# Undivided softmax weights, a four-block first modulation and a 12-tile ring in a two-block, four-layer network on one Trainium2 core

## The chip, the core and the metric

One core of one Trainium2 (trn2) chip runs the whole program. The core has a matmul engine (PE, with its weight loads PEld), three engines for everything elementwise (DVE, ACT, POOL), a queue engine (SP) from which every transfer of this kernel is issued, in order, and 16 DMA engines that serve it. The metric is the device time of one execution in microseconds (us), lower is better. Times below are medians of several runs or come from one profiled execution, and the text says which.

## What is computed

Two blocks, each of two layers, over a sequence of 1024 tokens of width 1024; in the first block also 256 context tokens. The change touches the first block: its modulations and its attention. Cut to those:

```
def hybrid_layer(xl, xc, c, c_ctx, w_mod, b_mod, ...):          # twice; the second without the context's update
    shift, scale, gate = split(silu(c) @ w_mod + b_mod, 3)       # 1024 -> 3072
    mod_c = silu(c_ctx) @ w_mod[:, :n] + b_mod[:n]
    hl = rms_norm(xl) * (1 + scale) + shift;   hc = the same of xc with mod_c
    pl = hl @ w_in;   pc = hc @ w_in
    a = conv_branch(...)                        # gated convolution of 31 taps
    b = windowed_attention(q, k, v, kc, vc, sink) * silu(b_gate)
    c = gated linear attention in chunks of 64
    xl = xl + gate * (concat(a, b, c) @ w_out)  # the context likewise in the first layer

def one_block(qn, kn, vn, mn):                  # 128 queries; 8 heads on 2 key heads
    s_loc = where(mn, qn . kn, -1e30);   s_ctx = qn . kc;   s_sink = sink
    p = softmax(concat([s_sink, s_ctx, s_loc]))
    return p_ctx . vc + p_loc . vn
```

The second block (gated spatial unit, pooling, retention, a feed-forward net with a short convolution) is untouched.

## The kernel before

Activations lie feature-major, [128 features, tokens], in three groups ("keys"): tokens 0 to 511, tokens 512 to 1023, and the 256 of the context. Projections are exact to float32 by splitting: each operand is a rounded part (`hi`) and a rest (`lo`), and each product is three matmuls of 512 columns (`mm3`, lines 226 to 228) over eight slices k of the inner dimension. A weight tile arrives as `wraw` (line 213, a ring of 3), ACT rounds it to `whi` (line 214), DVE makes `wlo` (line 201).

The program is written in stages, and a scheduler interleaves them: it fixes the order of the instructions of each engine and of SP's transfers when the program is built. On the chip every engine and every queue then works its list in that order, and waits where something isn't ready. Matmuls inside `in_order()` stay together.

**Start (`run`, lines 1653 to 1666).** SP loads the first key's eight `x` tiles. `mods` (lines 362 to 389) makes the modulation of layer 0: `w_mod` comes in tiles `wm` of 256 KB (line 374), and the matmul of line 375 adds each to the strip of 32 output rows of its block, so that the blocks of a group lie in different strips of one PSUM bank. Then the bank is copied to `mrow` (line 378), transposed (line 381), and biases are added (lines 385, 389) into `mc`. The blocks of layer 0 are taken in the order `MO` = 2, 0, 3, 1 in groups of `MG` = 2, with `WM` = 8 tiles in the ring. Blocks 2 and 0 hold scale and shift of the slices 0 to 3, so that after the first group `operands` (lines 1640 to 1650) can begin with four of the eight slices: `hi` on ACT (line 1647), the modulated `x` on POOL (line 1648), `lo` on DVE (line 1649). Then the first projections start.

**Attention (`attention`, `attend`, lines 866 to 958).** For each block of 128 queries and each of 2 key heads (20 iterations in layer 0, of which the first 4 are the context's; 16 in layer 1): the scores of 4 heads go to PSUM (matmuls of lines 897 and 908), DVE adds the mask, moves them to `P` and takes the maximum (lines 901, 911), ACT takes the exponential with its sum (line 918), DVE inverts the sums (`rsm`, line 920), and the weights are divided by them (line 926) on the engines that `NV` names: heads 0 and 2 on DVE, 1 and 3 on POOL. One iteration later (`LA` = 1) `attend` transposes `P` (line 940, four to a bank; copies to `pt` by lines 943 and 945 on DVE and ACT), multiplies by the values (line 954) into `po`, copies `po` to `ot` (line 957) and stores it (line 958). Transposes and `po` share the three banks of `psA`.

**Around it.** After `layer1(0, ...)` the text has the second call of `mods` (line 1669): eight blocks in two groups of four, with 4 tiles in the ring, and after that `out_proj`, which multiplies the stored branches `yl`, times the gates `gl`, by `w_out` (lines 974 to 993: two tiles each of `yl` and `gl` in the ring, the product on line 987, `yhi` on line 990). The scheduler had drawn the second modulation, and the first loads of `out_proj`, into the attention of layer 0. The pools of `mods` and of `out_proj` open in the same stretch of memory, one after the other.

Of the kernel before, what the change touches and what calls it, by code (L numbers as in the profile page):

```python
# [9 lines left out]
F32 = mybir.dt.float32  # L10
# [3 lines left out]
ALU = mybir.AluOpType  # L14
# [4 lines left out]
D = 1024  # L19
# [8 lines left out]
MO = (2, 0, 3, 1)  # L28
WM = 8
MG = 2  # L30
# [23 lines left out]
NV = "DPDP"  # L54
# [35 lines left out]
class Net:  # L90
# [270 lines left out]

    def mods(self, blocks, bufs=4, MG=4):

        nc = self.nc
        pool, tag = (self.psC, "sc") if blocks[0] == (0, 2) else (self.psB, "ax")
        with self.right(f"wm{blocks[0][0]}{blocks[0][1]}", bufs) as wm:
            for o in range(0, len(blocks), MG):
                grp = blocks[o:o + MG]

# [6 lines left out]
                n = 32 * len(grp)  # L376
# [489 lines left out]
    def attention(self, l, maskr, kh, vst):  # L866
        nc, tc, I = self.nc, self.tc, self.I
        with tc.tile_pool(name=f"at{l}", bufs=2, reuse_waits="tile") as ap:
            blocks = [("c", 0), ("c", 1)] if l == 0 else []
            blocks += [("l", i) for i in range(8)]  # L870
            late = []
            for kind, i in blocks:
# [8 lines left out]
                for v in range(2):  # L881
# [34 lines left out]
                    rs = self.sm.tile([128, 4], F32, name="rsm")  # L916
# [4 lines left out]
                    for h in range(4):  # L921
                        if NV[h] == "A":
                            nc.scalar.mul(P[:, h, :n], P[:, h, :n], rs[:, h:h + 1])
                            continue
                        eng = nc.vector if NV[h] == "D" else nc.gpsimd
                        eng.tensor_scalar(P[:, h, :n], P[:, h, :n], rs[:, h:h + 1], 1.0, op0=ALU.mult, op1=ALU.mult)
                    late.append(lambda v=v, i=i, P=P, nkt=nkt, lo_t=lo_t, yd=yd: self.attend(ap, vst, v, i, P, nkt, lo_t, yd))
# [5 lines left out]
    def attend(self, ap, vst, v, i, P, nkt, lo_t, yd):  # L933
# [15 lines left out]
        po = self.psA.tile([128, 512], F32, name="mm", tag="mm")  # L949
        with self.in_order():  # L950
            for kt in range(nkt):
                vt = kt if kt < 2 else 2 + lo_t + kt - 2
                for u in range(2):
                    nc.tensor.matmul(po[half[u], :256], vst[:, vt, 64 * v:64 * v + 64], PT[kt][:, u * 256:u * 256 + 256],  # L954
                                     start=kt == 0, stop=kt == nkt - 1)
        ot = ap.tile([128, 2, 128], F32, name="ot", bufs=2)
        nc.scalar.copy(ot, po[:, :256].rearrange("p (m t) -> p m t", m=2))
        nc.sync.dma_start(out=yd[2 + 2 * v:4 + 2 * v, :, i * 128:i * 128 + 128].rearrange("m p t -> p m t"), in_=ot)
# [647 lines left out]
    def run(self):  # L1606
# [7 lines left out]
        with self.norm_scratch("x0"), self.right("x0") as xp:  # L1614
# [40 lines left out]
            self.mods([(0, j) for j in MO], WM, MG)  # L1655
# [13 lines left out]
        self.mods([(0, 4), (0, 5), (1, 4), (1, 5)] + [(1, j) for j in range(4)])  # L1669
# [172 lines left out]
```

## Time and profile before

| | us |
|---|---|
| median of 3 runs (3587.53 to 3593.46) | 3589.61 |
| the profiled execution | 3592.81 |
| its span, first to last instruction | 3590.8 |
| PE busy in it | 3424.5 (95%) |
| DVE busy | 2487.3 (69%) |
| ACT busy | 1209.4 (34%) |
| POOL busy | 632.3 (18%) |

All times in rows are counted from the start of the span. "L375" is line 375 of the kernel; `out<-in` are the tiles; an arrow in brackets gives what ended the wait before an instruction. A float32 matmul of lines 375 and 954 shows as two records. Matmuls overlap, so their durations add up to more than the time they take: what one costs is read from the distance between starts. The granted clock of PE stands as a share of 2.4 GHz.

### The profile page before, as it was taken

What the parts mean: (1) busy time and instruction counts of PE and PEld (TensorE: products, weight loads), DVE (VectorE), ACT (ScalarE), POOL (GpSimd) and SP (SyncE); (2) the same over time, 40 slices, a digit from 0 to 9 for tenths busy, and PEclk for the clock granted to TensorE, in tenths of its full rate; (3) what the DMA queues carried; (4) which work ended last, traced back from release to release, by engine and by line L of the source; (5) the groups of instructions that cost most, each with busy time, mean ns of one, the idle gap of its engine ahead of it and who ended that gap; (6) DMA issues with size and microseconds to landing.
All of it is one profiled execution on the core that took longest, in us unless ns stands there. A gap on an engine that the chain in (4) does not pass through costs nothing.

```text
span 3590.8 us, 46973 instructions
## 1 busy us (share of the span) xinstructions
PE 3424.5 (95%) x17414; PEld 2727.1 (76%) x17414; DVE 2487.3 (69%) x3933; ACT 1209.4 (34%) x2189; POOL 632.3 (18%) x548
## 2 busy tenths in 40 slices
PE   7979999998989999999999998999999999999998
PEld 4868766787876677887788877887887878777786
DVE  5866568567665856455699999447354599999545
ACT  4114246341242642223343343214113343333322
POOL 4011332000214220130123231000030032322000
PEclk9989999999998999999999999999999999999999
DMA  6232355533124244315222223425323522221532
GB/s 204 71 82 67 112 165 168 169 123 95 58 78 119 71 124 138 97 42 184 80 97 77 82 77 110 140 82 160 91 61 114 159 74 77 77 82 63 179 100 91
DMA packets 245972, 380.70 MB, mean 106 GB/s; under 512 B 29104, under 2 KB 103792, under 8 KB 245232
## 3 DMA queue, kind: packets, MB, share of 16 engines
q1 hardware_dynamic: 245744, 377.71, 33.8%
q8 instruction: 137, 2.24, 0.3%
q14 instruction: 91, 0.75, 0.1%
HBM read 280.35 MB, written 97.26 MB: 105 GB/s over the span
## 4 chain that ended last, share of the span: by engine, by line
PE 68%; DVE 16%; issue 6%; DMA 4%; ACT 3%; POOL 2%; SPq 1%; DVEq 0%; POOLq 0%; ACTq 0%
PE mm L226 13%; PE mm L228 13%; PE mm L227 13%; PE ax L226 3%; PE ax L228 3%; PE ax L227 3%; PE sc L226 3%; PE sc L227 3%; PE sc L228 3%; DVE wlo L201 2%; DVE cv L1463 2%; PE mm L954 2%; PE mm L940 2%; DVE fth L347 1%; PE ax L715 1%
## 5 line engine op out<-in xcount | busy, mean ns | idle before, releaser
L226 PE MATMUL mm<-hi,whi 128*128 128x512 f32 (+1 forms) x1780 | 689.9, 388 | 28.3 <-ACT whi L214 13.1
L228 PE MATMUL mm<-hi,wlo 128*128 128x512 f32 (+1 forms) x1780 | 686.2, 386 | 9.0 <-DVE wlo L201 9.0
L227 PE MATMUL mm<-lo,whi 128*128 128x512 f32 (+1 forms) x1780 | 685.6, 385 | 1.4 <-DVE lo L1649 1.1
L214 ACT CAST whi<-wraw 128x512 fp32r<-128x512 f32 (+3 forms) x412 | 232.4, 583 | 598.7 <-PE mm L227 261.5
L226 PEld LDWEIGHTS mm<-hi,whi 128*128 128x128 f32 x1780 | 337.4, 190 | 100.3 <-ACT whi L214 14.4
L228 PEld LDWEIGHTS mm<-hi,wlo 128*128 128x128 f32 x1780 | 336.5, 189 | 83.7 <-DVE wlo L201 14.5
L227 PEld LDWEIGHTS mm<-lo,whi 128*128 128x128 f32 x1780 | 337.3, 189 | 72.8 <-DVE lo L1649 3.1
L201 DVE TENSOR_TENSOR wlo<-wraw,whi 128x512 fp32r<-128x512 f32 (+3 forms) x412 | 269.4, 670 | 176.3 <-ACT whi L214 174.9
L226 PE MATMUL sc<-hi,whi 128*128 128x512 f32 x732 | 287.9, 393 | 12.5 <-ACT whi L214 10.6
L228 PE MATMUL sc<-hi,wlo 128*128 128x512 f32 x732 | 287.7, 393 | 2.1 <-DVE wlo L201 1.9
L227 PE MATMUL sc<-lo,whi 128*128 128x512 f32 x732 | 287.2, 392 | 2.6 <-DVE lo L1649 2.5
L226 PE MATMUL mm<-whi,hi 128*128 128x512 f32 (+2 forms) x704 | 262.2, 372 | 28.2 <-ACT whi L214 28.2
L227 PE MATMUL mm<-wlo,hi 128*128 128x512 f32 (+2 forms) x704 | 257.6, 366 | 0.3
L228 PE MATMUL mm<-whi,lo 128*128 128x512 f32 (+2 forms) x704 | 257.1, 365 | 0.0
L188 POOL TENSOR_TENSOR rs<-rs,mhalf 128x4 f32<-128x4 f32 (+1 forms) x19 | 19.5, 1028 | 1073.7 <-DVE rs L183 1073.7
L498 DVE SCALAR_TENSOR_TENSOR ca<-u,wh,ca 128x1024 f32<-128x1024 f32 (+1 forms) x180 | 187.8, 1044 | 2.9
L226 PE MATMUL ax<-hi,whi 128*128 128x512 f32 x456 | 180.0, 395 | 4.7 <-DVE xn L1378 4.7
L228 PE MATMUL ax<-hi,wlo 128*128 128x512 f32 x456 | 179.7, 394 | 2.9 <-DVE wlo L201 2.9
L227 PE MATMUL ax<-lo,whi 128*128 128x512 f32 x456 | 179.1, 393 | 0.0
L201 DVE TENSOR_TENSOR wlo<-wr,whi 128x512 fp32r<-128x512 f32 x200 | 174.0, 881 | 0.0
L226 PEld LDWEIGHTS sc<-hi,whi 128*128 128x128 f32 x732 | 138.2, 189 | 44.0 <-ACT whi L214 11.3
L226 PEld LDWEIGHTS mm<-whi,hi 128*128 128x128 f32 x704 | 134.3, 191 | 47.4 <-ACT whi L214 29.0
(367 smaller groups left out, 6588.3 us busy)
## 6 DMA issues: line engine op xcount, KB each, us to landing
wr<-in_w_up SPq DMA_DIRECT2D x80, 512.0 KB, 3.6
wraw<-in_w_fm SPq DMA_DIRECT2D x108, 256.0 KB, 3.0
wm<-in_w_mod SPq DMA_DIRECT2D x96, 256.0 KB, 3.7
wraw<-in_w_down SPq DMA_DIRECT2D x96, 256.0 KB, 2.8
hid_d<-fth SPq DMA_DIRECT2D x44, 512.0 KB, 2.6
wraw<-hid_d SPq DMA_DIRECT2D x88, 256.0 KB, 2.9
wraw<-in_w_out SPq DMA_DIRECT2D x80, 256.0 KB, 3.4
yl<-y_d SPq DMA_DIRECT2D x64, 256.0 KB, 3.2
```

The source lines that it names most:

```text
L188: nc.gpsimd.tensor_tensor(out, out, e, op=ALU.pow)
L201: nc.vector.tensor_sub(out, x, f(hi))
L214: nc.scalar.copy(hi[:, c], r)
L226: nc.tensor.matmul(ps, sh, mh, start=start, stop=False)
L227: nc.tensor.matmul(ps, sh, ml, start=False, stop=False)
L228: self.mark = nc.tensor.matmul(ps, sl, mh, start=False, stop=stop)
L347: nc.vector.scalar_tensor_tensor(out, tanh_tmp, 1.0, x, op0=ALU.add, op1=ALU.mult)
L498: self.not_before(nc.vector.scalar_tensor_tensor(a, u[:, j:j + n], wh[:, c, j:j + 1], a, op0=ALU.mult, op1=ALU.add))
L715: nc.tensor.matmul(o_, a_, b_, start=first_, stop=last_)
L940: nc.tensor.transpose(pt[:, j * 128:j * 128 + 128], P[:, h, kt * 128:kt * 128 + 128], self.ident)
L954: nc.tensor.matmul(po[half[u], :256], vst[:, vt, 64 * v:64 * v + 64], PT[kt][:, u * 256:u * 256 + 256], start=kt == 0, stop=kt == nkt - 1)
L1463: nc.vector.scalar_tensor_tensor(t[:, o:], x[:, 0:S - o], wc(2 - o), t[:, o:], op0=ALU.mult, op1=ALU.add)
```

## The change

Three edits. (1) `attend` gets `rs`, the inverted sums. The division of line 926 is gone; instead POOL spreads `rs` to 64 columns for each head (`rw`), PE transposes that in two pieces into the free half of the bank of `po`, and DVE multiplies `ot` by it after ACT's copy. (2) `MG` is gone: the first modulation takes its four blocks as one group. (3) Both calls of `mods` get a ring of `WM` = 12 tiles (before: 8 and 4).

```diff
@@ -26,8 +26,7 @@
 W2 = (3, 1)
 W3 = ()
 MO = (2, 0, 3, 1)
-WM = 8
-MG = 2
+WM = 12
 LP_FFN = 1
 LAG_C = 3
 LAG_P = 4
@@ -51,7 +50,6 @@
 Y1B = 1
 QB = 3
 PB = 5
-NV = "DPDP"
 PBF = 4
 PD = (1, 3)
 RT = 2
@@ -359,13 +357,13 @@
         nc.vector.tensor_scalar_mul(self.cs[:, :, 0:2], th, 0.5)
         self.mc = [self.const.tile([128, 2, 24], F32, name=f"mc{l}") for l in range(2)]
 
-    def mods(self, blocks, bufs=4, MG=4):
+    def mods(self, blocks, bufs=4):
 
         nc = self.nc
         pool, tag = (self.psC, "sc") if blocks[0] == (0, 2) else (self.psB, "ax")
         with self.right(f"wm{blocks[0][0]}{blocks[0][1]}", bufs) as wm:
-            for o in range(0, len(blocks), MG):
-                grp = blocks[o:o + MG]
+            for o in range(0, len(blocks), 4):
+                grp = blocks[o:o + 4]
 
                 ps = pool.tile([128, 512], F32, name=tag, tag=tag)
                 for k in range(8):
@@ -913,24 +911,19 @@
                                     scalar=mx[:, 0, h:h + 1], op0=ALU.add, op1=ALU.max, accum_out=mx[:, 1, h:h + 1])
                     nm = self.sm.tile([128, 4], F32, name="nm")
                     nc.vector.tensor_scalar_mul(nm, mx[:, 1 if nl else 0, :], -0.125)
-                    rs = self.sm.tile([128, 4], F32, name="rsm")
+                    rs = self.sm.tile([128, 4], F32, name="rsm", bufs=6)
                     for h in range(4):
                         nc.scalar.activation(P[:, h, :n + 1], P[:, h, :n + 1], AF.Exp, scale=0.125, bias=nm[:, h:h + 1],
                                              accum_out=sums[:, h:h + 1])
                     nc.vector.reciprocal(rs, sums)
-                    for h in range(4):
-                        if NV[h] == "A":
-                            nc.scalar.mul(P[:, h, :n], P[:, h, :n], rs[:, h:h + 1])
-                            continue
-                        eng = nc.vector if NV[h] == "D" else nc.gpsimd
-                        eng.tensor_scalar(P[:, h, :n], P[:, h, :n], rs[:, h:h + 1], 1.0, op0=ALU.mult, op1=ALU.mult)
-                    late.append(lambda v=v, i=i, P=P, nkt=nkt, lo_t=lo_t, yd=yd: self.attend(ap, vst, v, i, P, nkt, lo_t, yd))
+                    late.append(lambda v=v, i=i, P=P, rs=rs, nkt=nkt, lo_t=lo_t, yd=yd: self.attend(
+                        ap, vst, v, i, P, rs, nkt, lo_t, yd))
                     if len(late) > LA[l]:
                         late.pop(0)()
             for x in late:
                 x()
 
-    def attend(self, ap, vst, v, i, P, nkt, lo_t, yd):
+    def attend(self, ap, vst, v, i, P, rs, nkt, lo_t, yd):
 
         nc = self.nc
         PT = []
@@ -947,7 +940,14 @@
         half = [slice(64 * u, 64 * u + 64) for u in range(2)]
 
         po = self.psA.tile([128, 512], F32, name="mm", tag="mm")
+
+        rw = ap.tile([128, 4, 64], F32, name="rw")
+        nc.gpsimd.tensor_copy(rw, rs.unsqueeze(2).broadcast_to([128, 4, 64]))
         with self.in_order():
+
+            for m in range(2):
+                nc.tensor.transpose(po[:, 256 + m * 128:384 + m * 128],
+                                    rw[:, 2 * m:2 * m + 2, :].rearrange("p h f -> p (h f)"), self.ident)
             for kt in range(nkt):
                 vt = kt if kt < 2 else 2 + lo_t + kt - 2
                 for u in range(2):
@@ -955,6 +955,7 @@
                                      start=kt == 0, stop=kt == nkt - 1)
         ot = ap.tile([128, 2, 128], F32, name="ot", bufs=2)
         nc.scalar.copy(ot, po[:, :256].rearrange("p (m t) -> p m t", m=2))
+        nc.vector.tensor_mul(ot, ot, po[:, 256:].rearrange("p (m t) -> p m t", m=2))
         nc.sync.dma_start(out=yd[2 + 2 * v:4 + 2 * v, :, i * 128:i * 128 + 128].rearrange("m p t -> p m t"), in_=ot)
 
 
@@ -1652,7 +1653,7 @@
 
             load(*groups[0])
             scale(*groups[0])
-            self.mods([(0, j) for j in MO], WM, MG)
+            self.mods([(0, j) for j in MO], WM)
             operands(*groups[0])
             weights = lambda *ms: [self.load_w(I["w_fm1"][0, m].rearrange("p k c -> p (k c)"), 1024) for m in ms]
             first = weights(*W1)
@@ -1666,7 +1667,7 @@
             operands(*groups[2])
         Hc = H.pop(2)
         self.layer1(0, mc, H, Hc, first)
-        self.mods([(0, 4), (0, 5), (1, 4), (1, 5)] + [(1, j) for j in range(4)])
+        self.mods([(0, 4), (0, 5), (1, 4), (1, 5)] + [(1, j) for j in range(4)], WM)
         H1, Hc1 = {}, []
 
         def fin0(key, X, acc):
```

The scheduler gives other orders to the engines. The first place is PE's list at the end of layer 0's attention. Before (`sc<-ks` are scores, `mm<-ident,P` the transposes of weights, `mm<-pt,vst` the products with values, `ax<-wm,cs` the second modulation, `ax<-yhi,whi` the first product of `out_proj`):

```order
L375 MATMUL ax<-wm,cs 32x512 x4
L954 MATMUL mm<-pt,vst 64x256 x2
L908 MATMUL sc<-ks_3749,qt 128x256
L908 MATMUL sc<-ks_3752,qt 128x256
L908 MATMUL sc<-ks_3749,qt 128x256
L908 MATMUL sc<-ks_3752,qt 128x256
L940 MATMUL mm<-ident,P 128x128 x16
L375 MATMUL ax<-wm,cs 32x512
L954 MATMUL mm<-pt,vst 64x256 x8
L375 MATMUL ax<-wm,cs 32x512 x2
L940 MATMUL mm<-ident,P 128x128 x3
L381 MATMUL ax<-ident,mrow 128x128
```

and in the changed kernel (line 373 is the modulation's matmul, 933 the transposes, 949 those of `rw`, 954 the products with values, 224 the first product of `out_proj`):

```order
L933 MATMUL mm<-ident,P 128x128 x16
L373 MATMUL ax<-wm,cs 32x512 x2
L949 MATMUL mm<-ident,rw 128x128 x2
L954 MATMUL mm<-pt,vst 64x256 x8
L933 MATMUL mm<-ident,P 128x128 x8
L373 MATMUL ax<-wm,cs 32x512 x4
L933 MATMUL mm<-ident,P 128x128 x8
L949 MATMUL mm<-ident,rw 128x128 x2
L954 MATMUL mm<-pt,vst 64x256 x8
L373 MATMUL ax<-wm,cs 32x512 x15
L379 MATMUL ax<-ident,mrow 128x128 x4
L373 MATMUL ax<-wm,cs 32x512 x32
```

Before, the 64 matmuls of the second modulation lay in groups of one to four all along the attention. Now 11 lie in its first iterations, none in the middle, and 53 (2, 4, 15 and 32) at its end, 47 of them behind its last product; `out_proj` comes after them.

The second place is SP's list at the same point. Before (`wm` are the modulation's tiles, `y_d<-ot` the stores of attention, `yl` and `gl` the loads of `out_proj`, `wraw<-in_w_out` its weights):

```order
L374 DMA wm<-in_w_mod 128x512 x3
L958 DMA y_d<-ot 128x2x128
L374 DMA wm<-in_w_mod 128x512
L983 DMA yl<-y_d 128x512 x2
L374 DMA wm<-in_w_mod 128x512 x3
L958 DMA y_d<-ot 128x2x128
L374 DMA wm<-in_w_mod 128x512
L986 DMA gl<-bg_d 128x512 x2
L374 DMA wm<-in_w_mod 128x512 x2
L958 DMA y_d<-ot 128x2x128
L374 DMA wm<-in_w_mod 128x512
L958 DMA y_d<-ot 128x2x128 x2
```

and in the changed kernel:

```order
L959 DMA y_d<-ot 128x2x128 x4
L372 DMA wm<-in_w_mod 128x512 x3
L959 DMA y_d<-ot 128x2x128
L372 DMA wm<-in_w_mod 128x512 x5
L959 DMA y_d<-ot 128x2x128
L372 DMA wm<-in_w_mod 128x512 x33
L211 DMA wraw<-in_w_out 128x512 x3
L984 DMA yl<-y_d 128x512
L987 DMA gl<-bg_d 128x512
L984 DMA yl<-y_d 128x512
L987 DMA gl<-bg_d 128x512
```

Before, the tiles alternated with the stores of attention and with loads of `out_proj`. Now 41 of the 64 come behind the 18th of the 20 stores, 33 of them behind the last one, and no load of `out_proj` is issued before them.

The third place is ACT's list after the first modulation's copy `mrow`. In the changed kernel (line 212 rounds the first weights, 1648 makes `hi` of a slice of key 0, 320, 323 and 1630 are squares of key 1):

```order
L376 COPY mrow<-sc 128x512
L212 CAST whi<-wraw 128x512 x2
L1648 ACTIVATE hi<-x_144,mc_125 128x512
L212 CAST whi<-wraw 128x512
L320 ACTIVATE nacc<-x_378 128x512
L1630 ACTIVATE nacc_377<-x_381 128x512
L1648 ACTIVATE hi<-x_147,mc_125 128x512
L323 ACTIVATE sq<-x_384 128x512
L212 CAST whi<-wraw 128x512
L1630 ACTIVATE sq_391<-x_389 128x512
L1648 ACTIVATE hi<-x_150,mc_125 128x512
```

Before, four `hi` stood between the two copies `mrow` and four behind the second; now all eight stand behind the one copy, with weights and squares between them.

## Rows read from the trace of the kernel before

**Rows 1.** The page, busy time: us, share of the span, instructions

```profile
PE 3424.5 (95%) x17414; PEld 2727.1 (76%) x17414; DVE 2487.3 (69%) x3933; ACT 1209.4 (34%) x2189; POOL 632.3 (18%) x548
```

**Rows 2.** Chain of waits, shares by line: attention of layer 0 (477 to 640), of layer 1 (1128 to 1280)

```profile
by line: PE mm L954 20.9%; PE mm L940 20.8%; PE ax L375 14.4%; PE sc L908 10.7%; PE sc L897 10.2%; DVE P L926 5.1%; issue 4.6%; DMA yl<-y_d 2.9%; DVE P L901 2.7%; DMA wm<-in_w_mod 2.0%; DVE P L911 1.9%; ACT pt L945 1.1%; POOL gms L188 0.6%;
...
by line: PE mm L954 17.9%; PE mm L940 16.6%; issue 12.0%; DVE P L926 9.6%; PE sc L897 7.4%; ACT P L918 7.3%; PE sc L908 5.1%; DVE P L901 4.1%; DVE P L911 3.5%; ACT pt L945 2.7%; DVE pt L943 2.1%; DMA qt<-qs_d 1.7%; PE ax L226 1.6%; POOL gms
```

**Rows 3.** Windows: stretch, length, busy of PE, PEld, DVE, ACT, POOL; clock; DMA share, GB/s

```profile
13.00:20.00 7.00, 6.52 (x20) 2.79 (x20) 1.15 (x3) 0.00 (x0) 2.45 (x2) 1.00 0.62 218
37.00:44.00 7.00, 5.42 (x16) 0.93 (x15) 0.68 (x1) 0.72 (x2) 0.00 (x0) 1.00 0.96 354
515.00:628.00 113.00, 110.95 (x761) 71.16 (x763) 93.41 (x285) 68.45 (x154) 23.62 (x35) 1.00 0.54 169
683.00:690.00 7.00, 4.50 (x14) 3.25 (x13) 3.32 (x6) 2.38 (x5) 0.00 (x0) 0.76 0.56 178
1128.00:1277.00 149.00, 137.60 (x978) 100.07 (x976) 122.27 (x378) 88.91 (x205) 34.31 (x49) 0.97 0.26 81
```

**Rows 4.** SP's queue in order of time, 0 to 62: start, us, what

```profile
6.37 29.54 SPq L374 DMA_DIRECT2D wm<-in_w_mod  x32
```

**Rows 5.** Waits of SP's queue, 0 to 62: total us, times, longest

```profile
SPq L374 <- PE sc L375: 12.7, 12, 3.8
...
SPq L374 <- DMA x<-in_xT: 2.5, 5, 1.2
```

**Rows 6.** PE in order of time, 12 to 45: start, us, what

```profile
12.84 1.89 PE L375 MATMUL sc<-wm,cs 128*32 128x512 f32 x2 [12.84 <-DMA wm<-in_w_mod]
...
38.79 4.41 PE L375 MATMUL sc<-wm,cs 128*32 128x512 f32 x12 [0.86 <-DMA wm<-in_w_mod]
...
44.44 0.50 PE L226 MATMUL sc<-hi,whi 128*128 128x512 f32 x1
```

**Rows 7.** DVE in order of time, 53 to 57

```profile
54.54 1.78 DVE L1649 TENSOR_TENSOR lo<-x,hi 128x512 fp32r<-128x512 f32 x1 [0.59 <-POOL x L1648]
```

**Rows 8.** Groups of instructions by shape, 490 to 640: busy us, mean ns, idle before

```profile
L926 DVE TENSOR_SCALAR P<-P,rsm 128x640 f32<-128x640 f32 x24 | 23.1, 1000 | 0.0
...
L926 POOL TENSOR_SCALAR P<-P,rsm 128x640 f32<-128x640 f32 x24 | 21.7, 917 | 47.7 <-DVE rsm L920 47.7
...
L957 ACT COPY ot<-mm 128x256 f32<-128x256 f32 x18 | 6.6, 368 | 20.7 <-PE mm L954 16.2 <-issue 4.4
...
L987 DVE SCALAR_TENSOR_TENSOR yl<-yl,gl 128x512 f32<-128x512 f32 x8 | 5.4, 684 | 1.9 <-DMA yl<-y_d 1.3 <-DMA gl<-bg_d 0.6
...
L990 ACT CAST yhi<-yl 128x512 fp32r<-128x512 f32 x8 | 5.0, 620 | 0.6 <-DVE yl L987 0.6
```

**Rows 9.** Chain in order of time, layer 0: products with values (start, us, what)

```profile
514.96 1.88 PE mm L954 x16
...
627.54 1.88 PE mm L954 x16
```

**Rows 10.** The same of layer 1

```profile
1164.41 2.31 PE mm L954 x20
...
1260.02 1.88 PE mm L954 x16
```

**Rows 11.** PE in order of time, end of layer 0's attention

```profile
630.38 1.07 PE L375 MATMUL ax<-wm,cs 128*32 128x512 f32 x8
...
632.54 1.99 PE L940 MATMUL mm<-ident,P 128*128 128x128 f32 x16
...
643.58 0.48 PE L226 MATMUL ax<-yhi,whi 128*128 128x512 f32 x1
...
659.57 0.39 PE L226 MATMUL ax<-yhi,whi 128*128 128x512 f32 x1
```

**Rows 12.** DMA issues, 480 to 640: count, KB each, median us to landing

```profile
wm<-in_w_mod SPq DMA_DIRECT2D x61, 256.0 KB, 3.7
...
yl<-y_d SPq DMA_DIRECT2D x10, 256.0 KB, 4.2
```

## The prediction

> **What bounds the kernel now.** I read five views, from the whole to the place. The page's busy times say that PE is the engine that matters: 3424.5 of 3590.8 us, with DVE next at 69% [rows 1]. That is an average, so the next views take the three places that the change touches. First the chain of waits of the two attentions: in layer 0 it consists almost wholly of PE's own work (lines 954, 940, 375, 908, 897), with only 5.1% on DVE's division; in layer 1 "issue" has 12.0% and the division 9.6% [rows 2]. Then the windows, which tell how full PE is there: 110.95 of 113 us in the loop of layer 0, 137.60 of 149 in layer 1 [rows 3]. So an instruction that leaves PE's list gives time back in layer 0; a shorter chain between engines can give back some 2 us there, and up to 11.4 in layer 1. Third, SP's queue and its waits at the start: the 32 tiles of the first modulation are issued over 29.54 us [rows 4], and 12.7 us of that SP waits for PE to free a slot of the ring of 8 [rows 5]; the 16 DMA engines are then 0.62 busy, against 0.96 at the second half's end [rows 3]. The start is bound by the transfers. Last, PE's list where the second modulation ends, which shows what has to be done before `out_proj`: nothing, its first product follows the last transposes at once [rows 11].
>
> **The first modulation (four blocks, ring of 12): -3.5 us, bounds -6.5 and 0.** A tile has 262,144 bytes: at the 354 GB/s of the end of the second half [rows 3] that is 0.74 us, and there PE takes six tiles in 4.41 us, 0.735 each [rows 6]. With 12 slots the transfers should run so from the first tile on: 12.84 + 31 x 0.735 + 0.3 for the last pair of matmuls = 35.9, where now the last group ends at 38.79 + 4.41 = 43.20 [rows 6]. From there to the first product it is 1.24 us now (44.44); the wider copy, four transposes and two weight casts ahead of the first `hi` add some 0.7 (a cast takes 0.62, rows of its kind in [rows 8]). The first product would start at 37.8, 6.6 us earlier. Against that stands ACT. Now four of the eight operands are made under the second group's transfers; afterwards all eight wait for the one copy, with squares and casts between them: 23 passes at 0.62 [rows 8] and four half passes at 0.4 (the copy of 256 columns takes 0.37 [rows 8]) make 15.9 us from 36.8 on, and the last `lo` follows some 1.4 us later, at 54.1. Now it ends at 54.54 + 1.78 = 56.3 [rows 7]. PE works through its first two products as the operands come, so the lead at the end lies between 2.2 and 6.5; I take 3.5, nearer the operands, since they come last. Nothing of it, the other end, holds if SP cannot have 12 transfers under way: it also waited 2.5 us for `x` to land, five times, before it issued tiles [rows 5].
>
> **The attention of layer 0: -15.4 us, bounds -22.7 and -14.4.** Line 375 has 14.4% of a chain of 163 us [rows 2], 23.5 us for 64 tiles, 0.37 each (four tiles in the end row take 1.07 [rows 11]). 53 of the 64 are moved behind or to the end of the loop: 19.4 us leave it. Two transposes of `rw` in each of 20 iterations come in: 16 take 1.99 [rows 11], 0.124 each, so 40 take +5.0. The division's 2 us of DVE in an iteration (640 columns, 1.00 us each; the other two heads on POOL at 0.92 [rows 8]) leave the way from the exponential to the transposes, but PE idles only 113 - 110.95 = 2 us there [rows 3], since each `P` is used one iteration later. I take -1, with 0 and the division's whole share of the chain, 5.1% of 163 = 8.3 us, as ends. POOL spreads `rw` (256 columns) in place of its two divisions of 640 at 0.92: no row shows that pass, so its price lies between nothing and 0.92, and as POOL was the idler engine and `rw` is wanted only an iteration later, I count it at nothing; without that cover it would cost PE a wait of up to 0.92 in an iteration. The last product with values then ends near 628 instead of 643.5.
>
> **The tail behind it: +32.6 us before `out_proj` begins.** In SP's list 33 tiles stand behind the last store. That store waits for ACT's copy (0.37 [rows 8]) and the new multiplication on DVE, which no row shows: half of a 512-column pass of 0.68 [rows 8] is its lower end, the whole pass its upper; I take 0.45. With two hops that is 1.0 us. The first of the 33 lands 3.7 us after its issue [rows 12], the others 0.72 to 0.74 apart, 32 x 0.72 = 23: they are all there at +27.7. PE's own work in this time is 47 tiles at 0.27, 12.6 us, so the transfers bound it. Behind them in SP's list come three `wraw`, then the first `yl` and `gl`: five more of the same size, 3.6 us, then the gate on DVE (0.68) and the cast on ACT (0.62) [rows 8]. 27.7 + 3.6 + 1.3 = +32.6, with PE's last modulation matmuls under them. 628.1 + 32.6 = 660.7, where now the first product starts at 643.58 [rows 11]. **Loop and tail together are +17.0** (rounded from 17.1), the largest term. If the issue is quicker than the row or the transfers begin before the store, it is some 5 less; at the 218 GB/s of the slow window [rows 3], a tile takes 1.2 us and it is some 15 more, which I take as unlikely, since nothing frees these slots late.
>
> **The ramp of `out_proj`: +6 us, ends 0 and 10; and +2 for the clock.** Now 20 loads of `yl` and `gl` were issued while attention ran [rows 12], and the products ran from the first at one matmul per 0.23 us (69 of them from 643.58 to 659.57 [rows 11]). Afterwards they start from nothing, in rings of two: a pair of slices needs landing 3.7, gate 0.68, cast 0.62 and again 0.68 for the rest, 5.7 us. Three more pairs after the first are 17.0 us, and the last pair's 12 matmuls at 0.23 end at +19.9. The first two products are 48 matmuls, 11.1 us without waits. That is 8.8 lost, 10 with a landing of 4.2 (the `yl` of [rows 12]); other work of PE's (the third accumulator's matmuls) fills some, so 6. PE will have idled: in the window at 683 it works 4.50 of 7 us and its granted clock is 0.76 [rows 3], a mean between 1.2 and 2.4 GHz. At half the rate a matmul costs 0.23 us more; for about ten of them I add 2.
>
> The Trainium skill ("TensorE: Matmul & The Clock Gate", section "HAM oscillation") has a rule that speaks against this edit: bursts of matmuls separated by waits for a DMA start at the lower clock every time. The window at 683, whose bursts stand behind waits, agrees with it. By that rule all 36 matmuls of the three later pairs would run so, 8 us in place of 2 by the 0.23 each, and the sum would be +23.5.
>
> **Layer 1's attention: -4 us, bounds -7.4 and +4.** No modulation lies there. Periods on the chain are (1260.02 - 1164.41) / 11 = 8.69 us [rows 10], against 9.38 in layer 0 ((627.54 - 514.96) / 12, [rows 9]). DVE, busy 122.27 of 149 us [rows 3], loses two passes of 0.9 to 1.0 in each of 16 iterations and gains one of 0.45. PE pays 32 x 0.124 = 4.0 for the new transposes. Of its 11.4 idle us I take 8 back, since the division's share of the chain there, 9.6% of 152 = 14.6 us [rows 2], would cover them all but the exponential's 7.3% stays. -8 + 4 = -4; all idle time back is -7.4, none +4.
>
> **The sum.** Start -3.5, loop and tail +17.0, ramp +6, clock +2, layer 1 -4: **+17.5 us**. The profiled execution took 3592.81 us (span 3590.8), 3.2 more than the median of 3589.61; against the median the forecast is 3589.6 + 17.5 = **3607 us**.
>
> **Rivals.**
> *Even.* The start keeps its whole 6.5, layer 1 gets back all 7.4, and the ramp is covered by other products, with no clock lost: 17 - 6.5 - 7.4 = +3, 3593. For it speaks that layer 1's idle time is real; against it that the operands come last at the start, and that no load of `out_proj` is issued before the tail. Chance 17%.
> *Faster: the loops are paced by the division.* If it is the round from exponential over division to transposes that sets the period, and PE's fullness is only matmuls stretched to it, each of 36 iterations falls by the 1.0 us of a division: 17.5 - 36 = -18.5, 3571. It decides from a fall of 0.69 us per iteration (0.5 would just balance the 17.5) beyond what I count: then the result is faster by more than the bound. For it: the division has 9.6% of the chain in layer 1. Against: 110.95 of 113 us busy in layer 0. Chance 7%.
> *Worse tail.* Tiles behind the last store land at the 0.62 busy share of the start and the ramp runs at the lower clock: +17.5 + 10 to 15, some 3619. For it: the queue's own wait of five `x` tiles [rows 5]; against it: 0.96 busy at 37 to 44 [rows 3]. Chance 15%.
> *The ring does nothing at the start.* Where SP can't have more than about eight transfers under way, the first edit brings 0 and the sum is +21, 3611; this lies in the forecast's own range.
>
> **How the numbers follow.** The forecast has 61% and its own range is 3597 to 3617, from the bounds of start (3 each way), ramp (6, 4) and layer 1 (3, 8). With "even" and "worse tail" the range is 3590 to 3621; "faster" and the outer tails stay outside. A measurement of this kernel can tell 0.2%, 7.2 us: faster 0.07, same 0.17, slower 0.76.
>
> **What would show it.** First product near 38 and last `lo` near 54 at the start; the last product with values near 628; the 33rd tile landing 28 us behind, PE mostly idle with SP's tiles in a row at 0.72; first product of `out_proj` near 661; periods of layer 1 near 8.4; no wait for line 926. The prediction is wrong if SP's 33 tiles start ahead of the last store, if `out_proj` begins before 650, or if periods fall by 0.7 us or more.

## The result, and the profile after

The changed kernel takes 3611.22 us (median of 5 runs, 3604.0 to 3616.28) against 3589.61 for the kernel before: ratio 1.0055, 95% interval 1.0038 to 1.0073. It is slower, by 21.6 us on the medians, or 0.55% by the ratio, where +17.5 and 3607 were forecast. The terms of the sum did not come out nearly as well as the sum. The profiled execution is one of 3611.22, its span 3609.3 against 3590.8.

The page's busy times of the changed kernel, to set beside [rows 1]:

```profile
PE 3459.7 (96%) x17482; PEld 2754.4 (76%) x17482; DVE 2436.8 (68%) x3897; ACT 1212.6 (34%) x2188; POOL 588.5 (16%) x512
```

DVE has lost 50 us and POOL 44, as the division is gone. PE has 68 recorded matmuls more and is busy 35 us longer.

The windows of the changed kernel (columns as in [rows 3]): the start, the stretch of the first products, the tail behind layer 0's attention, the ramp of `out_proj`, and 70 us of layer 1's loop.

```profile
13.00:20.00 7.00, 6.25 (x20) 2.87 (x20) 1.59 (x3) 0.24 (x1) 2.69 (x3) 1.00 0.92 337
45.00:60.00 15.00, 11.73 (x36) 8.69 (x36) 9.25 (x13) 10.97 (x21) 12.05 (x9) 0.73 0.67 231
625.00:655.00 30.00, 28.29 (x98) 5.86 (x90) 2.70 (x8) 2.37 (x5) 0.00 (x0) 1.00 1.01 358
655.00:675.00 20.00, 12.81 (x39) 7.19 (x39) 11.03 (x22) 6.37 (x11) 0.00 (x0) 0.91 0.78 263
1180.00:1250.00 70.00, 70.00 (x544) 57.31 (x541) 55.58 (x205) 51.41 (x117) 5.60 (x19) 1.00 0.26 78
```

The same two stretches of the kernel before, layer 1's loop and the first products:

```profile
1180.00:1250.00 70.00, 66.63 (x471) 48.63 (x470) 61.66 (x187) 45.22 (x102) 16.76 (x25) 1.00 0.26 80
45.00:60.00 15.00, 12.75 (x54) 8.97 (x53) 12.39 (x15) 11.74 (x22) 8.45 (x7) 1.00 0.66 217
```

The tail stands plainly at 625 to 655: the DMA engines are 1.01 busy at 358 GB/s, and PE's 28.29 us of "busy" are 98 records, 0.29 us each, where eight of the same kind take 1.07 us [rows 11], 0.13 each: they wait for tiles (PE busy counts a matmul that stretches). Layer 1's loop shows the opposite: 544 matmuls in 70 us where there were 471 (about 19 of the 73 more are the new transposes), although PE looked 95% busy before. The column beside it, the weight loads (PEld), showed more room: 48.63 us busy before, 57.31 after.

PE in order of time in the changed kernel, at the start and around the tail (start, us, what, and in brackets the idle time before it):

```profile
20.33 4.39 PE L373 MATMUL sc<-wm,cs 128*32 128x512 f32 x24
...
28.28 9.80 PE L373 MATMUL sc<-wm,cs 128*32 128x512 f32 x28 [1.08 <-DMA wm<-in_w_mod]
38.76 0.66 PE L379 MATMUL sc<-ident,mrow 128*128 128x128 f32 x4 [0.68 <-ACT mrow L376]
40.73 0.50 PE L224 MATMUL sc<-hi,whi 128*128 128x512 f32 x1 [1.31 <-ACT hi L1648]
...
622.86 1.95 PE L954 MATMUL mm<-pt,vst 128*64 128x256 f32 x16
624.73 6.89 PE L373 MATMUL ax<-wm,cs 128*32 128x512 f32 x28
...
634.91 20.45 PE L373 MATMUL ax<-wm,cs 128*32 128x512 f32 x64
656.08 0.66 PE L379 MATMUL ax<-ident,mrow 128*128 128x128 f32 x4 [0.73 <-ACT mrow L376]
660.48 0.49 PE L224 MATMUL ax<-yhi,whi 128*128 128x512 f32 x1 [3.74 <-ACT yhi L991]
```

SP's queue over the same two places:

```profile
7.52 24.49 SPq L372 DMA_DIRECT2D wm<-in_w_mod  x32
...
626.71 0.38 SPq L959 DMA_DIRECT2D y_d<-ot  x1
627.18 22.05 SPq L372 DMA_DIRECT2D wm<-in_w_mod  x33
```

All 33 tiles are issued behind the last store, in 22.05 us (0.67 each), and the first product of `out_proj` starts at 660.48, where the prediction had 660.7. At the start the tiles are issued in 24.49 us in place of 29.54 [rows 4], and the first product comes at 40.73 in place of 44.44 [rows 6], but not at 37.8.

**Where the time went.** Each kernel's trace has 12744 matmuls of exact products; I compare when the n-th starts, and for layer 1 the first and last product with values. The last column repeats this for two traces taken on one chip (the first two experiments).

| stretch | forecast | after against before | the same, one chip |
|---|---|---|---|
| start, to the 301st | -3.5 | +0.7 | -0.1 |
| layer 0's attention, tail and ramp (1651st to 2101st) | +25 | +23.2 | +23.0 |
| layer 1's loop, first to last product with values | -4 | -13.9 | -15.8 |
| everything else | 0 | +8.6 | +18.6 |
| last product | +17.5 | +18.6 | +25.7 |

So the largest term held, layer 1 gained three to four times what was forecast, and a loss of 9 to 19 us stands where no line was edited.

### The profile page after: what moved, and what is told of

Its sections match the earlier page's. It is cut to its first block, busy times and chain, and to the rows that moved or that the text cites. A ratio compares the mean times of both kernels' runs of the same rounds, so it can differ in the third digit from the quotient of the medians.

```text
span 3609.3 us, 47132 instructions
## 1 busy us (share of the span) xinstructions
PE 3459.7 (96%) x17482; PEld 2754.4 (76%) x17482; DVE 2436.8 (68%) x3897; ACT 1212.6 (34%) x2188; POOL 588.5 (16%) x512
## 4 chain that ended last, share of the span: by engine, by line
PE 77%; DVE 9%; issue 5%; DMA 3%; ACT 2%; POOL 2%; SPq 1%; DVEq 0%; POOLq 0%; ACTq 0%
PE mm L225 14%; PE mm L224 14%; PE mm L226 14%; PE sc L224 4%; PE sc L226 4%; PE sc L225 4%; PE ax L225 4%; PE ax L226 4%; PE ax L224 4%; PE mm L954 2%; PE mm L933 2%; PE sc L906 1%; DVE wlo L199 1%; PE ax L713 1%; PE sc L895 1%
## 5 line engine op out<-in xcount | busy, mean ns | idle before, releaser
L225 PE MATMUL mm<-lo,whi 128*128 128x512 f32 (+1 forms) x1780 | 693.0, 389 | 1.0 <-DVE lo L1650 0.7
```

What stands on the lines that cost most here:

```text
L225: nc.tensor.matmul(ps, sh, ml, start=False, stop=False)
```

## The experiments

**Is the loss elsewhere the chip's?** The kernel before and the changed one, unedited, profiled on one chip.

> The kernel before, as it is, so that its trace and the next one's come from one chip. In the two traces at hand the matmuls of 512 columns of the untouched second block stand 229 ns apart before and 232.4 ns after, and between 1550 us and the end the changed kernel loses 9 us more without any edit there. Theory 'chip': the 3.4 ns belong to the chip that a run fell on; here this kernel and the changed one show the same distance, whichever it is. Rival 'kernel': the change moved the tiles in memory; here 229 again and the changed one 232 again. The time is that of the kernel before, ratio 1.000.

> The changed kernel, as it is. By 'chip' (see the run before) its distance of matmuls is that of the kernel before on this chip, the second block's +9 us shrinks to 0, and the ratio is 1.003. By 'kernel' the distance is 232 against 229 and the ratio 1.005 or more. In both: first product of out_proj near 660, layer 1's periods 7.47 us.

Measured: 0.9995 (0.9977 to 1.0014) and 1.0044 (1.0026 to 1.0063). Windows of 100 us in the second block, where PE works without a pause on matmuls of 512 columns, tell the distance by the count. The kernel before, then the changed one:

```profile
2320.00:2420.00 100.00, 100.00 (x438) 82.06 (x437) 43.96 (x72) 21.31 (x40) 0.00 (x0) 1.00 0.32 92
```

```profile
2320.00:2420.00 100.00, 100.00 (x432) 81.09 (x431) 44.69 (x75) 22.46 (x42) 0.00 (x0) 1.00 0.33 95
```

438 against 432 matmuls, both at granted clock 1.00; in the middle of such stretches they start 229 ns and 232.4 ns apart. "Chip" falls: the distance comes with the kernel. The ratio alone would not have told, as its interval holds both the 1.003 of "chip" and the 1.005 of "kernel".

**The undivided weights alone, and the changed kernel with the small ring.** The first takes all but the weights back, the second only the second modulation's ring (edits against the changed kernel, cut to the calls; the first does both, and both keep its 6 small tiles for the sums, of which more below):

```diff
-            self.mods([(0, j) for j in MO], WM)
+            self.mods([(0, j) for j in MO], 8, 2)
...
-        self.mods([(0, 4), (0, 5), (1, 4), (1, 5)] + [(1, j) for j in range(4)], WM)
+        self.mods([(0, 4), (0, 5), (1, 4), (1, 5)] + [(1, j) for j in range(4)])
```

> The kernel before with the undivided weights alone (rings of 8 and 4 tiles, two groups of two blocks). In its order 47 of the 64 matmuls of the second modulation stand behind the last product with values as in the changed kernel, but among the first products of out_proj, and the loads of out_proj alternate with the tiles. Theory: what the change gains comes from this edit: layer 1's periods fall to 7.47 (21 us less there) and layer 0's attention ends some 20 us earlier; the tail costs only PE's own 47 x 0.27 = 12.7 us, since the transfers lie beside products. Sum 21 + 20 - 13 = 28 us less, some 3562, ratio 0.992. Rival: with four tiles PE waits for each group of transfers (3.7 us landing for 4 tiles, 12 groups, 44 us), and the tail is as long as in the changed kernel: layer 1's 21 us less, layer 0 even or +20: ratio 0.994 to 1.000.

> The changed kernel with the second modulation's ring back at 4 tiles; the first modulation stays as changed (four blocks, 12 tiles). Theory: the cost of the change is this ring, which lies over the memory of out_proj's loads; taking it back gives 23 + 13 us: some 3562 to 3565, ratio 0.993, and differs from the undivided weights alone by the first modulation's part only, which in the trace is worth between -3.7 us (first product) and +0.7 (150 matmuls later). Rival: the tail stands behind the attention by the undivided weights themselves, and the ring does nothing: ratio 1.003 or more.

Measured: 1.0033 (1.0017 to 1.0050) and 1.0046 (1.0029 to 1.0064). My theory missed in both. Layer 1's loop fell by 15.8 us in each (21 expected), but layer 0 with its ramp was +24 and +29 us against the kernel before on the same chip (counted as in the table). SP's queue of the undivided weights alone, behind the attention:

```profile
637.13 5.75 SPq L372 DMA_DIRECT2D wm<-in_w_mod  x4
642.93 0.42 SPq L984 DMA_DIRECT2D yl<-y_d  x1
645.33 4.08 SPq L372 DMA_DIRECT2D wm<-in_w_mod  x4
649.46 0.42 SPq L984 DMA_DIRECT2D yl<-y_d  x1
651.88 4.32 SPq L372 DMA_DIRECT2D wm<-in_w_mod  x4
...
680.36 4.31 SPq L372 DMA_DIRECT2D wm<-in_w_mod  x4
```

With four tiles the transfers go round by fours, some 6 us a round, and each round holds up the loads of `out_proj` behind it until 684. So the ring of 12 is not what makes the tail: it is the place that the scheduler gives the second modulation once the weights are undivided, behind the attention, whatever the ring. The kernel without the division, further below, has a ring of 4 and the tail too: +20 in the same stretch.

**The place of the tiles.** The change also gives the inverted sums 6 small tiles in place of 4. That moves everything allocated after them by 64 bytes. I tried the number alone, in the kernel before (6, 12 and 8) and in the changed kernel (20); no instruction moves in any of the four.

```diff
-                    rs = self.sm.tile([128, 4], F32, name="rsm")
+                    rs = self.sm.tile([128, 4], F32, name="rsm", bufs=6)
```

> The kernel before with one number changed: the small tiles of the inverted sums get 6 places instead of 4, as in the changed kernel. No instruction changes and none moves; every tile allocated after them lies 64 bytes further on in each partition (the operands hi from 62464 to 62528). Theory 'place': this is why all kernels with undivided weights run their matmuls of 512 columns at 232.4 to 233.4 ns apart where both traces of the kernel before show 229: here 232.4 too, and as in the kernel after against the one before some 3 us in layer 0's first half and 10 from layer 1's end on: +10 to +15 us, ratio 1.003 to 1.004. Rival: the distance belongs to the edits themselves (other engines reading beside PE): 229, ratio 1.000.

> The changed kernel with 20 such places instead of 6: no instruction changes, and the tiles behind lie 512 bytes further on than in the kernel before, so at the same remainder of 512 as there. Theory 'place': 229 ns in the second block, 10 to 15 us less than the changed kernel, ratio to the kernel before 1.000 to 1.002. Rival: 232.4 ns and 1.0044 as the changed kernel beside this run's reference.

> The kernel before with 12 places for the inverted sums: the tiles behind lie 256 bytes further on, no instruction moves. 64 bytes cost 3.4 ns per matmul of 512 columns; 512 cost nothing. If what counts is the place in 512 bytes, the distance is 232.4 ns here too and the time 10 to 17 us more (1.003 to 1.005); if it is the place in 256 bytes or less, 229 ns and ratio 1.000.

> The same with 8 places, 128 bytes further on. 229 ns if the place in 128 bytes counts, 232.4 if that in 256 or 512 does.

Measured: 1.0066 (1.0042 to 1.0090) for 64 bytes in the kernel before; 1.0007 (0.9994 to 1.0020) for 256; 3597.47 us in a single run for 128, beside a median of 3590.38. The changed kernel with 512 bytes: 1.0024 (1.0005 to 1.0043). The same window as above, for the kernel before with 64, 256 and 128 bytes and the changed kernel with 512, in this order:

```profile
2320.00:2420.00 100.00, 100.00 (x433) 81.03 (x431) 44.70 (x75) 22.22 (x42) 0.00 (x0) 1.00 0.32 95
```

```profile
2320.00:2420.00 100.00, 100.00 (x438) 82.00 (x438) 43.72 (x72) 20.09 (x38) 0.00 (x0) 1.00 0.30 89
```

```profile
2320.00:2420.00 100.00, 100.00 (x431) 80.56 (x430) 45.17 (x74) 22.54 (x42) 0.00 (x0) 1.00 0.31 95
```

```profile
2320.00:2420.00 100.00, 100.00 (x438) 82.05 (x437) 45.13 (x74) 22.33 (x42) 0.00 (x0) 1.00 0.32 95
```

433, 438, 431, 438: a shift by 256 or 512 bytes costs nothing here, one by 64 or 128 bytes costs 1.1 to 1.6% of the matmuls of this stretch. "Place" holds; of the four shifts, those that leave the remainder by 256 as it was are free. The price in time is less sure: +24 us by the ratio in the kernel before (four runs; more than the 1.003 to 1.004 expected), 7 us by the two ratios of the changed kernel, 1.0044 as it is and 1.0024 with 512 bytes (two chips, with intervals that overlap). From the 5001st to the 7001st product, where DVE is busy 95.5 of 100 us (1880 to 1980), the shift of 64 bytes costs nothing: 482.1 us, and 482.2 in the kernel before.

**The ring of 12 alone**, in the kernel before:

```diff
-        self.mods([(0, 4), (0, 5), (1, 4), (1, 5)] + [(1, j) for j in range(4)])
+        self.mods([(0, 4), (0, 5), (1, 4), (1, 5)] + [(1, j) for j in range(4)], 12)
```

> The kernel before with the second modulation's ring at 12 tiles alone. Its 64 matmuls stay spread over layer 0's attention, but the loads of out_proj's operands come behind the last stores, as the ring lies over their memory. Theory: the ring by itself costs only the ramp of out_proj, 5 to 10 us at its start: ratio 1.0015 to 1.003. Rival: the ring makes the tail: 20 us or more, ratio 1.005.

Measured: 1.0039 (1.0026 to 1.0052), 14 us: over what I had for the ramp, and the rival's 1.005 lies inside the interval, so the time alone doesn't decide. The trace does: layer 0 with the ramp is +5 against the trace of the kernel before in the first experiment, which is the ramp without a tail. The other 9 us stay open; the profiled execution is the fastest of the ten (3596.68 us) and ends only 5.5 us behind that trace.

**What the division cost layer 1.** First the division left out, with nothing in its place (the output isn't scaled by the sums); then all four divisions of an iteration on POOL.

```diff
-NV = "DPDP"
+NV = "PPPP"
```

> The kernel before without the division and without anything in its place: the weights stay undivided and the result isn't scaled. It prices the two transposes of rw with the rest of the new work: layer 1's loop, first to last product with values, takes 107 us with the undivided weights and 121.6 to 122.7 with the division. Theory 'PE': after the change PE sets the period, and the transposes cost their own 15 x 0.31 = 4.6 us: 102.5 here. Rival: they lie in waits: 107. The second modulation stands at the end of layer 0's attention here as in the changed kernel, so the tail of some 22 us is here too.

> The kernel before with all four divisions of an iteration on POOL (3.7 us there) and none on DVE. It tells apart what the division cost layer 1: DVE's time (2 of the 7.6 us that DVE works in a period of 8.1) or the way through the division that the transposes wait for. Theory 'DVE': POOL idles in the loop, so its 3.7 us fit, and the loop falls from 122 to 107 plus or minus 3, less the 4.6 of the transposes of rw that aren't there. Rival 'way': the transposes wait longer, for 3.7 instead of 2 us, and the loop stays at 122 or grows.

Measured, one run each: 3605.95 and 3582.64 us beside a median of 3590.38. The groups of the products with values in layer 1 give the loop (count, min/median/max ns, first and last start): the kernel before and the changed one on one chip, without the division, with the division on POOL (the last two on another chip).

```profile
L954 PE MATMUL mm<-pt,vst x304: 379/379/582, 1144.0 to 1268.4; 128*64 128x256 f32 x152
```

```profile
L954 PE MATMUL mm<-pt,vst x304: 379/379/431, 1176.0 to 1284.6; 128*64 128x256 f32 x152
```

```profile
L948 PE MATMUL mm<-pt,vst x304: 379/379/431, 1170.8 to 1281.2; 128*64 128x256 f32 x152
```

```profile
L954 PE MATMUL mm<-pt,vst x304: 379/379/431, 1144.5 to 1264.9; 128*64 128x256 f32 x152
```

124.4 us, 108.6, 110.4 and 120.4. Over all experiments, six traces with the division as before give 123.1 to 124.4, six with the undivided weights and their new transposes 108.6 to 109.2. Without the division the loop is no shorter than with the transposes of `rw` in it, so those transposes cost nothing that shows in layer 1; my "PE" theory of 4.6 us falls (the two lists are ordered differently, so they lie in waits or the order pays for them, which these runs don't part). With DVE free of the division and POOL doing it, a fifth to a quarter of the gain is there (2.7 to 4.0 us), and the chain of waits says what holds the rest. Shares by line, 1165 to 1255, for the kernel before, the one with POOL, and the changed one:

```profile
by line: PE mm L954 20.8%; PE mm L940 19.8%; DVE P L926 14.0%; PE sc L897 7.8%; issue 7.3%; ACT P L918 6.3%; PE sc L908 5.8%; DVE P L901 4.7%; DVE P L911 4.3%; DVE pt L943 3.3%; ACT pt L945 2.7%; DVE rsm L920 1.1%; PE ax L226 0.5%; DVE mx L
```

```profile
by line: PE mm L940 23.6%; PE mm L954 21.7%; POOL P L926 19.6%; PE sc L897 8.4%; PE sc L908 7.8%; DVE P L901 4.5%; issue 4.2%; DVE P L911 2.0%; ACT P L918 2.0%; ACT pt L945 1.9%; PE ax L227 0.8%; DVE rsm L920 0.7%; DVE ylo L201 0.7%; DVE mx
```

```profile
by line: PE mm L933 28.6%; PE mm L954 27.3%; PE sc L906 22.4%; PE sc L895 14.8%; PE mm L949 2.7%; DVE P L899 1.1%; POOL gms L186 1.1%; issue 0.9%; POOL ggt L721 0.7%; PE mm L729 0.5%; PE ax L224 0.3%; DVE mx L899 0.2%; DVE nm L913 0.1%
```

The division is on the chain with 14.0% on DVE and 19.6% on POOL; without it over 96% of the chain is PE. So neither theory by itself: the transposes waited for the division on whichever engine it ran (the way), and DVE's 2 us are the smaller part.

**The best version.** Undivided weights, the first modulation as before, 4 places for the sums, and the second modulation written into layer 0's loop:

```diff
+            steps = self.mods_steps([(0, 4), (0, 5), (1, 4), (1, 5)] + [(1, j) for j in range(4)]) if l == 0 else None
...
-                    P = ap.tile([128, 4, 641], F32, name="P", bufs=PBF)
+                    P = ap.tile([128, 4, 641], F32, name="P", bufs=PBF - (l == 0))
...
                     if len(late) > LA[l]:
                         late.pop(0)()
+                    if steps:
+                        next(steps, None)
```

(`mods_steps` is `mods` with a `yield` after each slice; its call after `layer1` is gone.)

> Undivided weights with 4 places for the inverted sums (tiles where the kernel before has them), the first modulation as before, and the second modulation written into layer 0's attention by hand: after each block of queries and key head the four matmuls of one slice, with a ring of 4 tiles (a P tile less, 3, makes room). In its order the matmuls lie in groups of four among the scores again, and 19 of the loads of out_proj are issued before the last store. Theory: the tail was the cost of the changed kernel, and it comes from the order alone: layer 0 ends as in the kernel before or some 2 us earlier (21 us less for the weights, 19 back for the matmuls in the loop), layer 1's 21 us remain: -20 to -25 us, ratio 0.993 to 0.9945. Rival: with the matmuls back in the loop the undivided weights gain nothing in either layer because PE is full: ratio 1.000.

Measured: 3578.3 us, ratio 0.9971 (0.9958 to 0.9985). It beats both kernels, by half of what I expected. Its products with values in layer 1, and PE and SP where layer 0 ends:

```profile
L964 PE MATMUL mm<-pt,vst x304: 379/379/431, 1150.4 to 1259.0; 128*64 128x256 f32 x152
```

```profile
629.18 0.40 PE L224 MATMUL ax<-yhi,whi 128*128 128x512 f32 x1
...
638.32 1.95 PE L964 MATMUL mm<-pt,vst 128*64 128x256 f32 x16
```

The loop takes 108.6 us, the whole gain; the first product of `out_proj` starts at 629.18, before the last products with values. In the table's terms, against the trace of the kernel before in the first experiment (another chip), layer 0 is +1 and layer 1's loop -15.7. So the tail is gone, and of the 21 us expected of layer 1 its loop gives 16. What else is missing the traces don't tell: the stretch from the 2101st to the 3651st product, in which the loop lies, is 9 us shorter against that trace and 14 against the other one of the kernel before, as those two differ by 5 there.

## Why the prediction was right, and where it wasn't

The direction, the range and the largest term held. That the time fell where it was forecast is luck: layer 1 took 10 to 12 us less than forecast, the start 3 to 4 more, and the stretches without an edit, priced at nothing, 9 to 19 more. One of the prediction's own signs of being wrong came: periods in layer 1 fell by more than 0.7 us, from 8.69 to 7.47.

- **Layer 0, tail and ramp: +25 forecast, +23 measured.** The mechanism is the one given: SP's 33 tiles behind the last store, transfers at 0.67 us each, PE waiting. Inside it two sizes were off and made up for each other. The loop ended at 624.7, where the next matmul starts, not at 628.1, though the 1651st product ahead of it came 3 us later than before: counted from there it fell by 21.7, not 15.4. Part of it is the price of the two transposes in an iteration, 5.0 in the sum: from the first to the last product with values this loop takes 132.4 us, and 130.4 without the division and without them. From there to `out_proj` it took 35.7 us in place of 32.6: the tiles behind the last store were issued 2.4 us after the last product (1.0 taken), had been used 28.2 after that (26.7), and the first product followed 5.1 later (4.9). The ramp lost 9 us (8 with the clock).
- **The clock in the ramp: +2 forecast, 1.5 measured.** In 655 to 675 the granted clock is 0.91. Behind the wait of 3.74 us PE runs at the lower of its two levels: the eight matmuls from 661.20 to 664.60 take 3.4 us in place of 1.9. Behind the later waits of at most 0.91 us the matmuls follow at the full clock: two of them are 0.72 us long in the second row below, 1.06 in the first. The Trainium skill's rule ("TensorE: Matmul & The Clock Gate", section "HAM oscillation"), by which bursts behind waits for a DMA start at the lower clock every time, was priced at 8 us for the three later pairs; the trace doesn't show it for them. Where the clock cost more was the start, and no term had it there: 0.73 in 45 to 60, with PE waiting for operands, and between 43 and 61 fourteen matmuls of the first products stand 0.43 us apart in place of 0.23, 2.8 us in all. The rows of the ramp:

```profile
663.07 1.06 PE L225 MATMUL ax<-ylo,whi 128*128 128x512 f32 x2
...
671.14 0.72 PE L224 MATMUL ax<-yhi,whi 128*128 128x512 f32 x2 [0.91 <-ACT yhi L991]
```

- **The start: -3.5 forecast, 0 measured.** The step "nearer the operands, since they come last" was right, but the operands were priced on ACT alone, and on an ACT that never waits: 54.1 for the last `lo`. It ended at 62.54 + 1.22 = 63.8. Of these 9.7 us ACT itself has 6.0: its last `hi` ended at 57.90 + 0.81 = 58.7, not at 36.8 + 15.9 = 52.7. It began at 38.12, its `hi` take 0.8 us where 0.62 was taken, and its list holds casts of weights and squares of the next key, for whose tiles it waited 3.8 us in all (one `x`, issued at 41.10, landed at 47.2 and stands on the chain). The other 3.7 come behind the last `hi`: POOL, which I left out, is busy 12.05 of 15 us in 45 to 60, against 8.45 before. It has the eight modulated `x` and the squares' sums of the next key in one queue, and `lo` waits for it, as it already did in [rows 7]. Nor did the transfers of the tiles run through at 0.735. They moved 382 GB/s and more up to 19; then the ring of 12 was full, as PE had spent 14.9 to 20.33 on lines 292 and 302 but for three tiles, and in 19 to 21 it was 96 GB/s. The last tile was used at 28.28 + 9.80 = 38.1, not at 35.9. The rows of ACT and POOL, of DVE, of the chain of waits, and the windows of the transfers:

```profile
57.90 0.81 ACT L1648 ACTIVATE hi<-x,mc 128x512 fp32r<-128x512 f32 x1
...
52.84 4.05 POOL L1649 TENSOR_SCALAR x<-x,mc 128x512 f32<-128x512 f32 x2
...
60.78 1.73 POOL L1649 TENSOR_SCALAR x<-x,mc 128x512 f32<-128x512 f32 x1
```

```profile
60.12 1.22 DVE L1650 TENSOR_TENSOR lo<-x,hi 128x512 fp32r<-128x512 f32 x1 [1.69 <-POOL x L1649]
...
62.54 1.22 DVE L1650 TENSOR_TENSOR lo<-x,hi 128x512 fp32r<-128x512 f32 x1
```

```profile
41.57 5.66 DMA x<-in_xT
...
48.75 1.65 POOL nacc L1632
50.41 1.21 POOL x L1649
...
51.65 1.77 DVE lo L1650
```

```profile
17.00:19.00 2.00, 2.00 (x9) 0.60 (x8) 0.16 (x1) 0.00 (x0) 1.03 (x1) 1.00 1.03 382
19.00:21.00 2.00, 2.00 (x11) 0.92 (x12) 0.56 (x1) 0.00 (x0) 0.00 (x0) 1.00 0.37 96
```

- **Layer 1: -4 forecast (bounds -7.4 and +4), -13.9 and -15.8 measured.** The step that failed is "of its 11.4 idle us I take 8 back": it took busy time as work. In 1180 to 1250 PE was busy 66.63 of 70 us with 471 matmuls; the same 70 us hold 544 now. What an iteration's matmuls need is read off the distances between starts (20 products in 2.31 us [rows 10], 16 transposes in 1.99 [rows 11], and so on for the scores), and by that the loop of 8.69 us a period had over a microsecond of waits in each: after the change a period of 7.47 is nearly all PE's work, the new transposes included. The rival "the loops are paced by the division" was right for layer 1, at about 1 us an iteration, and had 7%. The 4.0 us for new transposes were not there either (110.4 us without them). The changed kernel's chain, products with values, 7.47 us a period:

```profile
1200.21 2.31 PE mm L954 x20
...
1207.66 2.31 PE mm L954 x20
...
1215.13 2.31 PE mm L954 x20
```

- **Everything else: 0 forecast, +8.6 and +18.6 measured.** No step spoke of it. The place of the tiles is shown to make the distance 232 ns, and the traces say that it makes most of this sum. Counted in the same way against the first experiment's trace, six kernels whose operands lie as before or 256 or 512 bytes on have -5.7 to +1.0 here (the other trace of the kernel before, 256 bytes, the changed kernel with 512, the ring of 12 alone, the division on POOL, the best version), and six that are moved by 64 or 128 bytes have +3.4 to +18.6. That it makes all of the sum isn't shown: the kernel without the division, not moved, has +8.4, and the changed kernel itself +9.0 in one trace and +18.6 in the other.
- **Rivals.** "Even" and "worse tail" did not come; "faster" came in layer 1 alone. The first edit does next to nothing at the start, though not for want of transfers under way (0.92 busy in 13 to 20, 0.62 before).

## What to carry to other kernels

Taking work off the chain between engines can move other work: look where the scheduler puts what used to fill the gaps, and if it ends up in a tail, write it back into the loop by hand. Price a loop by counting its instructions and the distance between their starts, not by busy time, which counts a stretched matmul as work. And when a kernel gets slower in stretches that nobody edited, compare the addresses of the tiles too: two small tiles more cost some 7 us here by one pair of ratios and 24 by another, which is of the size of the edits that the change is named after.

## What was not expected of the hardware

A matmul of 512 columns of float32 in an unbroken run takes 229 ns when its operands' tiles lie where the kernel before has them or 256 or 512 bytes further on, and 232.4 to 233.3 when 64 or 128 bytes further, at granted clock 1.00 throughout. The weights' tiles (`whi`, `wlo`) of the ring did not move, as their pool opens ahead of that of the sums, and the operands `hi` and `lo` did; that it is these reads is argued, not tried. And the place is not all: some kernels with their tiles in the good place had a stretch at the slow distance all the same, as the ring of 12 alone and here the changed kernel with 512 bytes, 430 matmuls in 100 us, where the kernel before has 439:

```profile
1880.00:1980.00 100.00, 100.00 (x430) 81.03 (x429) 95.44 (x106) 40.80 (x57) 29.38 (x17) 1.00 0.24 79
```

What sets it there stays open.
